# FFN activations of a decoder block turned by 16-bit transposing DMAs in place of TensorE transposes

## The chip, the cores and the metric

The kernel runs on one core of a Trainium2 chip. The metric is the time of one execution on the device, in microseconds (us), as the median of three runs. TensorE (PE) multiplies matrices, VectorE (DVE) and ScalarE (ACT) work elementwise, and the queue of SyncE (SP) and that of ScalarE issue the DMA transfers. Every engine works off its own list in the order of the program; semaphores order the engines among each other.

## The reference

One layer of a hybrid decoder for 256 positions and a model width of 2048, in float32: a mixer (dilated sliding-window attention beside a gated linear recurrence) and a SwiGLU feed-forward network (FFN), each between two RMSNorms and added to the residual stream. The part that matters here is the FFN, with D_FF = 5632:

```python
a = rmsnorm(h, norm_ffn_pre[layer])
gt, up = jnp.split(a @ w_ffn_gate_up[layer], [D_FF], axis=-1)
ff = (jax.nn.silu(gt) * up) @ w_ffn_down[layer]
h = h + rmsnorm(ff, norm_ffn_post[layer])
```

The product `silu(gt) * up` comes out with positions on the partitions. It has to be turned, so that its 5632 channels lie on the partitions, before it can be multiplied with `w_ffn_down`.

## The kernel before

**Split products.** Every float32 product is made of three in a faster format: each operand is split into a high part, rounded to that format by a ScalarE copy, and a low part, the difference, made by VectorE. Each block of weights therefore passes through raw buffers (tag `raw`, 3 buffers, loaded by SP's queue), a ScalarE copy and a VectorE subtraction before TensorE can use it. Some steps use sums of weights and of activations ("by seven", seven products where eight stand otherwise); their splitting takes more instructions: lines 434 to 449 with the sums made in place, lines 425 to 430 with sums made ahead of time and fetched from DRAM (`s<-presum`).

**Items.** The program is one list of items; an item is one step of a wide block. For item i the main loop calls `prepare(i)`, which emits the splitting of item i + 2, the fetch of sums for item i + 4 and the weight load for the raw slot five items on (its buffer comes free when the split of item i + 2 has read it), then `multiply(i)`, then pieces of the evacuations. All of it is unrolled when the program is built, so that this order is the order on each engine's list.

**Gate and up.** Block j of eleven makes 512 channels of the gate and the same 512 of up: four banks of 128 positions x 512 channels, in eight steps c = 0 to 7 (orders `GATE_UP3` and `GATE_UP4`; steps 2, 4, 5 and 6 of the latter are by seven). Each step is 21 or 24 products of 128x128 by 128x512. After the last step by seven `gather` moves the partial sums into four float32 tiles `e` (128x512 each, tag `e`, 6 buffers), `b.rest`. When the block is done, `evac_ffn` (lines 1402 to 1412) adds the banks to them, applies Silu to the gate's two and multiplies up's two by them (line 1411). The two products, one for each half of the positions, are appended to the deque `turns`. For block 0 `evac_first` does the same with tiles `g` and `u`.

**The turn.** After step c = 1 of the following gate/up block (`turn=1`; for the last product after step 3 of the first down block) the main loop calls `turn_act` (lines 1365 to 1379, from line 1653). It turns the product by eight TensorE transposes of 128x128 in float32 against an identity matrix, into two PSUM banks; ScalarE copies each bank into `act`, a slot of the pool `r` (16 slots); ScalarE's queue stores it to DRAM (`acts`). There are eleven turns. The down blocks fetch the tiles back (line 1386, 22 times 512 KB) and split them.

**Other queues.** `turns` also holds the generators that turn the mixer's output earlier in the program; the main loop tells these from the FFN's products by their type (line 1655). SP's queue carries all weight loads, the fetches of sums and the fetches of `act`, in program order; a DMA that waits for its buffer or its data holds back those behind it.

Of the kernel before, what the change touches and what calls it, by code (L numbers as in the profile page):

```python
# [14 lines left out]
F32 = mybir.dt.float32  # L15
F32R = mybir.dt.float32r
I32 = mybir.dt.int32
AF = mybir.ActivationFunctionType
OP = mybir.AluOpType

P = 128
S = 256
# [78 lines left out]
def tile_hybrid_block(ctx: ExitStack, tc: tile.TileContext, t, out):  # L101
    nc = tc.nc
# [12 lines left out]
    def nm(s):  # L115
        serial[0] += 1
        return f"{s}_{serial[0]}"

    def rslot(s):
        return rpool.tile([P, 1024], F32R, tag="r", bufs=16, name=nm(s))  # L120
# [4 lines left out]
    def aux():  # L125
        return auxp.tile([P, 512], F32, tag="aux", name=nm("aux"))

    def acc_bank():
        return accp.tile([P, 512], F32, tag="acc", name=nm("acc"))

    def p3(s, dtype, n, bufs, tag=None):
        return wide_pool[-1].tile([P, n], dtype, tag=tag or s, bufs=bufs, name=nm(s))
# [7 lines left out]
    def rsqrt_mean(dst, ss, n, bias=None):  # L140
# [6 lines left out]
        bias = bias or (eps[:, 0:1], eps[:, 1:2])  # L147
        nc.scalar.activation(y, ss, AF.Ln, scale=1.0 / n, bias=bias[0])
        nc.scalar.activation(y, y, AF.Exp, scale=-0.5)
        nc.vector.tensor_scalar(v, ss, -0.5 / n, bias[1], op0=OP.mult, op1=OP.add)  # L150
# [15 lines left out]
    ident = cpool.tile([P, P], F32, name="ident")  # L166
# [68 lines left out]
    def both_halves(ev, i):  # L235
        def go(banks):
            s = ptile("sum").rearrange("p (h t) -> p h t", h=2)
            for n, ps in enumerate(banks):
                nc.scalar.activation(s[:, n, :], ps[:, S:], AF.Copy)
            for n, ps in enumerate(banks):  # L240
# [86 lines left out]
    def ahead_of_time():  # L327

        if fp and back and not hold[0]:
            advance(back)  # L330
# [6 lines left out]
    def prepare(i):  # L337
        split(i + AHEAD)
        fetch_sums(i + AHEAD + 2)
        if i + AHEAD < len(items):  # L340
            load_upto(items[i + AHEAD][2] + N_RAW)

    def multiply(i):
        kind, n = items[i][:2]
        if kind is chunks:
            multiply_chunk(n)
            return
        b, c = steps[n][:2]

        def between():  # L350
            if b.mid:
                b.mid(c)
                prepare(i)
            advance_lanes()

        multiply_wide(n, between=between)
# [4 lines left out]
    def split_chunk(j):  # L361
        raw, w = chunks[j][2], wslot()
        chunks[j][3:] = wh, wl = w[:, :1024], w[:, 1024:]
        nc.scalar.activation(wh, raw, AF.Copy)  # L364
        nc.vector.tensor_sub(wl, raw, wh.bitcast(F32))  # L365

    def split_first(n, at):
# [5 lines left out]
        c = slice(at * 512, (at + 1) * 512)  # L373
        nc.scalar.activation(hi[:, c], raw[:, c], AF.Copy)
        nc.vector.tensor_sub(lo[:, c], raw[:, c], hi[:, c].bitcast(F32))
# [25 lines left out]
    def split_wide(n):  # L401
# [5 lines left out]
        if (b, i) == spare:  # L407
            hi = p3("spare", F32R, 2048, 1, "sum")
            lo = Joined(p3("spare", F32R, 1536, 4, "d"), p3("spare", F32R, 512, 4, "d"))
            nc.scalar.activation(hi, raw, AF.Copy)  # L410
            for c in (slice(0, 1536), slice(1536, 2048)):
# [94 lines left out]
    def gather(b):  # L506

        e = {k: p3("e", F32, 512, 6) for k in ((0, 1), (1, 1), (0, 0), (1, 0))}
        x = b.bank
        nc.scalar.activation(e[0, 1], x["p1"], AF.Copy)  # L510
        nc.vector.tensor_add(e[1, 1], x["p6"], e[0, 1])
        nc.vector.tensor_add(e[0, 0], x["p5"], e[1, 1])
        nc.vector.tensor_add(e[1, 0], x["p7"], e[0, 0])
        nc.vector.tensor_add(e[1, 1], x["p7"], e[1, 1])
        b.rest = e
# [129 lines left out]
        return row[:, None, :].to_broadcast([P, n, S])  # L645

    evacs, turns, lanes, queue = deque(), deque(), [deque(), deque()], deque()
    back, hold = deque(), [False]
    ready = set()

    def advance(q):
        if q:
            try:
                next(q[0])
            except StopIteration:
                q.popleft()
                return

    def flush(q):
        while q:  # L660
            advance(q)
# [3 lines left out]
    def advance_lanes():  # L665
        tick[0] += 1
        for lane in lanes:
            if not lane and queue:
                lane.append(attention())
            advance(lane)  # L670
# [305 lines left out]
    def recurrence(half):  # L976
# [31 lines left out]
        def on_diagonal(c, ps):  # L1008
            nc.vector.copy_predicated(
                at[:, c * 512 : (c + 1) * 512].rearrange("p (e t) -> p e t", e=4),  # L1010
                ident[:, None, :].to_broadcast([P, 4, P]).bitcast(I32),
                ps.rearrange("p (e t) -> p e t", e=4),
# [25 lines left out]
        for lev, w in enumerate(LEVELS):  # L1038
# [10 lines left out]
            if w < 32:  # L1049
                nc.vector.copy_predicated(  # L1050
                    at[:rows].rearrange("p (e n w) -> p e n w", e=8, w=2 * w)[:, :, :, w:],
                    lmask[:rows, lev, :].rearrange("p (n w) -> p n w", w=w)[:, None, :, :]
                    .to_broadcast([rows, 8, 64 // w, w]).bitcast(I32),
                    ps[:rows].rearrange("p (e n w) -> p e n w", e=8, w=w),
# [305 lines left out]
    def eslot(s="e"):  # L1360
        return p3(s, F32, 512, 6, "e")
# [2 lines left out]

    def turn_act(u):

        x = rslot("act").bitcast(F32)
        dst = x.rearrange("p (k t) -> p k t", k=4)
        for i in range(2):
            ps = aux() if now[0].flip else acc_bank()  # L1370
            for kk in range(2):
                for s in range(2):
                    at, c = kk * S + s * P, (2 * i + kk) * P
                    nc.tensor.transpose(ps[:, at : at + P], u[s][:, c : c + P], ident)  # L1374
            nc.scalar.activation(
                dst[:, 2 * i : 2 * i + 2, :], ps.rearrange("p (k t) -> p k t", k=2), AF.Copy
            )
        act_t.append(dram.tile([P, 1024], F32, name=nm("acts")))
        nc.scalar.dma_start(act_t[-1], x)

# [8 lines left out]
    now = [None]  # L1389

    def evac_first(b):
        while "r2" not in ready:
            yield
        g, u = ([eslot(n) for _ in range(2)] for n in ("g", "u"))
        for s in range(2):
            nc.scalar.activation(g[s], b.bank[s, 0], AF.Silu, scale=r2c[:, s : s + 1])
        yield
        for s in range(2):
            nc.vector.tensor_mul(u[s], b.bank[s, 1], g[s])
        turns.append(u)  # L1400

    def evac_ffn(b):
        e, x = b.rest, b.bank
        for key in ((0, 0), (0, 1), (1, 0), (1, 1)):
            nc.vector.tensor_add(e[key], x[key], e[key])
            s, g = key
            if g == 0:
                nc.scalar.activation(e[key], e[key], AF.Silu, scale=r2c[:, s : s + 1])
        yield
        for s in range(2):  # L1410
            nc.vector.tensor_mul(e[s, 1], e[s, 1], e[s, 0])
        turns.append([e[0, 1], e[1, 1]])


    fss, fz, fpost, parts_of, a7 = [], {}, [], {}, {}
# [153 lines left out]
    for half in range(2):  # L1569
        for g in range(3):  # L1570
            c = 1024 * g + 512 * half
# [24 lines left out]
    w = t["w_ffn_gate_up"][0]  # L1596
    spare = None
    add_wide_block(w, (0, FF), PLAIN, lambda k: hT[0](k), None, evac_first, True, mid=more_h)
    spare = wides[-1], 0
    for j in range(1, 11):  # L1600
        add_wide_block(w, (512 * j, FF + 512 * j), GATE_UP4 if j > 1 else GATE_UP3, lambda k: hT[0](k),
                       lambda m: h7[m], evac_ffn, j % 2 == 0,
                       pre=begin_wides if j == 1 else None, turn=1)
# [22 lines left out]
    for i in range(len(items)):  # L1626
        kind, n, _ = items[i]
        b, c = kind[n][:2]
        wide = kind is steps
        if wide:  # L1630
            now[0] = b
        if c == 0 and b.pre:
            b.pre()
        if not wide and n in items_pre:
            items_pre[n]()
        if together <= i < together + 5:
            if i == together:
                flush(evacs)
                mix_to_ffn(i)
            continue  # L1640
        if not (wide and b.mid):
            prepare(i)
        if i >= len(items) - 3:
            continue
        multiply(i)
        if b.post:
            b.post(c)
        if wide and c == b.last7:
            gather(b)
        advance(evacs)  # L1650
        if wide and c == b.turn:
            flush(evacs)
            turn_act(turns.popleft())
        for _ in range(2):
            if turns and type(turns[0]) is not list:
                advance(turns)
        advance_lanes()
        if not wide:
            ahead_of_time()
        if c == (len(b.order) if wide else b.steps) - 1:  # L1660
            evacs.append(b.evac(b if wide else b.banks))
            if wide:
                advance(evacs)
# [63 lines left out]
```

## Time and profile before

| what | value |
|---|---|
| median of three runs | 1697.17 us (1697.14 to 1698.39) |
| profiled execution, from the first to the last instruction (its span; its own time beyond that isn't given) | 1695.7 us |
| granted TensorE clock, mean | 0.998 |
| DMA, mean over the span | 244 GB/s, 413.49 MB |
| line 1374, TensorE transposes | 88 of 270 to 273 ns |
| line 1375, ScalarE copies of the turned banks | 22, median 594 to 596 ns |
| line 1379, stores of the turned tiles | 11 of 512 KB |
| line 1411, the products of gate and up, on VectorE | 20 (blocks 1 to 10), 684 ns |
| line 287, loads of gate/up weights | 156 of 512 KB and 20 of 256 KB |

The profile gives, for each engine, the instructions by source line with their shapes, and for each group the idle time of the engine just before it and what ended that idle time ("<-PE aux L138": an instruction of TensorE, line 138, that wrote a tile called `aux`). PEld is TensorE's loading of the stationary operand, which runs beside the products. "SPq" and "ACTq" are the DMA issues of these engines' queues; the time to landing of a DMA runs from its issue to its last byte. The chain that ended last is followed backwards from the end: at each step to what released an instruction, or to the one before it on the same engine. Matmuls overlap, so that one which takes 390 ns in its row may start 227 ns after the one before.

### The profile page before, as it was taken

The numbers are of one execution on the slowest core, as the hardware profiler recorded it, in microseconds if no ns is written. First come the engines' busy times: TensorE is split into PE (matmuls) and PEld (weight loads), VectorE is DVE, ScalarE is ACT, GpSimd is POOL, SyncE is SP. The second block draws the span as 40 slices with busy tenths as digits, with TensorE's granted clock in tenths as the row PEclk, the third lists the DMA queues.
The fourth block names the chain that finished last, engine by engine and source line by source line (L and its number), as shares of the span: only waits on it lengthen the run. The fifth ranks groups of instructions, "written<-read, shape, count | busy, mean of one in ns | idle before, by whom it ended". The sixth has DMA issues, their size and how long they took to land.

```text
span 1695.7 us, 21719 instructions
## 1 busy us (share of the span) xinstructions
PE 1684.4 (99%) x8257; PEld 1415.9 (83%) x8257; DVE 1416.2 (84%) x1623; ACT 945.6 (56%) x1080; POOL 3.8 (0%) x13
## 2 busy tenths in 40 slices
PE   9999999999999999999999999999999999999997
PEld 7888888888888888888888888888888888888886
DVE  6999888867978987776668888888888888898987
ACT  6655555544455555555545547555555555665653
POOL 0000000000000000000000000000000000000000
PEclk9999999999999999999999999999999999999999
DMA  8567666669677766788857646777777777777673
GB/s 286 204 224 243 231 232 229 234 216 316 228 250 256 261 239 215 259 310 279 291 171 276 208 165 226 270 249 251 255 254 255 250 248 272 252 269 259 238 255 130
DMA packets 228905, 413.49 MB, mean 244 GB/s; under 512 B 12816, under 2 KB 79552, under 8 KB 226240
## 3 DMA queue, kind: packets, MB, share of 16 engines
q1 hardware_dynamic: 218544, 373.93, 65.6%
q10 hardware_dynamic: 10192, 38.15, 5.9%
q8 instruction: 64, 1.05, 0.3%
q14 instruction: 41, 0.34, 0.1%
q0 software_dynamic: 64, 0.02, 0.0%
HBM read 376.92 MB, written 35.13 MB: 243 GB/s over the span
## 4 chain that ended last, share of the span: by engine, by line
PE 98%; DVE 1%; ACT 0%; issue 0%; DVEq 0%; ACTq 0%
PE acc L138 62%; PE aux L138 34%; PE aux L943 0%; PE aux L610 0%; PE aux L1374 0%; DVE fz L1501 0%; PE acc L1374 0%; DVE wl L420 0%; ACT junk L1455 0%; PE aux L597 0%; DVE e L1451 0%; ACT w L418 0%; PE aux L1136 0%; PE aux L1246 0%; DVE yT L578 0%
## 5 line engine op out<-in xcount | busy, mean ns | idle before, releaser
L138 PE MATMUL acc<-xT,w 128*128 128x256 f32 (+1 forms) x2048 | 365.1, 338 | 0.0
L420 DVE TENSOR_TENSOR wl<-raw,w 128x2048 fp32r<-128x2048 f32 (+1 forms) x140 | 304.6, 2183 | 70.5 <-ACT w L418 68.7
L138 PEld LDWEIGHTS acc<-xT,w 128*128 128x128 f32 x2048 | 311.9, 188 | 44.7
L365 DVE TENSOR_TENSOR w<-raw,w 128x1024 fp32r<-128x1024 f32 x176 | 215.1, 1223 | 118.1 <-ACT w L364 117.5
L418 ACT ACTIVATE w<-raw 128x2048 fp32r<-128x2048 f32 (+1 forms) x140 | 254.6, 1827 | 104.4 <-PE aux L138 33.6
L364 ACT ACTIVATE w<-raw 128x1024 fp32r<-128x1024 f32 x176 | 185.8, 1058 | 191.9 <-PE acc L138 135.8
L138 PE MATMUL acc<-w,xT 128*128 128x512 f32 x578 | 168.8, 391 | 0.0
L439 ACT ACTIVATE w<-sum 128x1024 fp32r<-128x1024 f32 x57 | 60.6, 1062 | 184.8 <-DVE sum L434 177.6
L138 PE MATMUL acc<-w,hT 128*128 128x512 f32 x472 | 152.7, 391 | 0.4 <-DVE hT L1258 0.4
L447 DVE TENSOR_TENSOR wl<-sum,w 128x1024 fp32r<-128x1024 f32 x114 | 137.2, 1221 | 12.8 <-ACT w L439 12.8
L138 PEld LDWEIGHTS acc<-w,xT 128*128 128x128 f32 x578 | 108.2, 188 | 22.2
L138 PE MATMUL aux<-w,hT 128*128 128x512 f32 x374 | 120.0, 389 | 0.0
L449 DVE TENSOR_TENSOR dl<-raw,dh 128x1536 fp32r<-128x1536 f32 x57 | 100.1, 1757 | 14.3 <-ACT dh L445 13.0
L138 PE MATMUL aux<-w,xT 128*128 128x512 f32 x344 | 109.8, 389 | 0.0
L138 PEld LDWEIGHTS acc<-w,hT 128*128 128x128 f32 x472 | 88.5, 188 | 19.0 <-DVE hT L1258 0.9
L138 PE MATMUL acc<-wl,hT 128*128 128x512 f32 x236 | 91.9, 389 | 0.0
L445 ACT ACTIVATE dh<-raw 128x1536 fp32r<-128x1536 f32 x57 | 84.1, 1476 | 8.0 <-PE aux L138 4.4
L138 PE MATMUL acc<-w,a 128*128 128x512 f32 x268 | 83.6, 389 | 0.0
L138 PEld LDWEIGHTS aux<-w,hT 128*128 128x128 f32 x374 | 70.2, 188 | 14.5
L138 PE MATMUL acc<-w,so 128*128 128x512 f32 x240 | 80.8, 391 | 0.0
L138 PE MATMUL aux<-w,a 128*128 128x512 f32 x254 | 79.4, 389 | 0.0
L138 PEld LDWEIGHTS aux<-w,xT 128*128 128x128 f32 x344 | 64.6, 188 | 13.4
(299 smaller groups left out, 2976.2 us busy)
## 6 DMA issues: line engine op xcount, KB each, us to landing
raw<-in_w_in SPq DMA_DIRECT2D x270, 512.0 KB, 4.8
raw<-in_w_ffn_gate_up SPq DMA_DIRECT2D x156, 512.0 KB, 4.9
raw<-in_w_ffn_down SPq DMA_DIRECT2D x88, 512.0 KB, 5.5
pre<-in_w_ffn_gate_up SPq DMA_DIRECT2D x40, 512.0 KB, 6.5
presum<-pre ACTq DMA_DIRECT2D x20, 1024.0 KB, 4.7
s<-presum SPq DMA_DIRECT2D x40, 512.0 KB, 6.9
raw<-in_w_mix_out SPq DMA_DIRECT2D x32, 512.0 KB, 4.8
act<-acts SPq DMA_DIRECT2D x22, 512.0 KB, 6.6
```

The source lines that it names most:

```text
L138: nc.tensor.matmul(ps, lhsT, rhs, start=start, stop=stop, skip_group_check=True)
L364: nc.scalar.activation(wh, raw, AF.Copy)
L365: nc.vector.tensor_sub(wl, raw, wh.bitcast(F32))
L418: nc.scalar.activation(hi[:, c], raw[:, c], AF.Copy)
L420: nc.vector.tensor_sub(lo[:, c], raw[:, c], hi[:, c].bitcast(F32))
L439: nc.scalar.activation(hi[:, :1024], s[:, :1024], AF.Copy)
L445: nc.scalar.activation(dhi, d, AF.Copy)
L447: nc.vector.tensor_sub(lo[:, c], s[:, c], hi[:, c].bitcast(F32))
L449: nc.vector.tensor_sub(dlo, d, dhi.bitcast(F32))
```

## The change

`turn_act` uses TensorE and PSUM no longer. A float32 word is taken as two 16-bit halves. ScalarE copies the halves of each product, viewed as unsigned 16-bit numbers, apart: into the gate's two tiles, which have been read by then, so that the first 512 columns hold one half of every word and the next 512 the other. Four transposing DMAs on SP's queue, 128 partitions x 512 halves (128 KB) each, write them turned into the product's own two tiles, one tile for each half of the words. Two steps later ScalarE joins the halves in `act`, and the store follows as before. For this `turn_act` becomes a generator with two bare yields, which a new deque `turned` advances once per step; the evacuations append a pair of lists (the tiles to be reused and the product), and the test in the main loop asks for a tuple.

```diff
+U16 = mybir.dt.uint16
...
-    back, hold = deque(), [False]
+    back, turned, hold = deque(), deque(), [False]
...
     def turn_act(u):

+        flat, turned = u
+        for s in range(2):
+            nc.scalar.activation(
+                flat[s].bitcast(U16).rearrange("p (z c) -> p z c", z=2),
+                turned[s].bitcast(U16).rearrange("p (c z) -> p z c", z=2), AF.Copy,
+            )
+        for s in range(2):
+            for z in range(2):
+                nc.sync.dma_start_transpose(
+                    turned[z].bitcast(U16).rearrange("p (k t) -> p k t", k=4)[:, :, s * P : (s + 1) * P],
+                    flat[s].bitcast(U16)[:, z * 512 : (z + 1) * 512],
+                )
+        yield
+        yield
         x = rslot("act").bitcast(F32)
-        dst = x.rearrange("p (k t) -> p k t", k=4)
-        for i in range(2):
-            ps = aux() if now[0].flip else acc_bank()
-            for kk in range(2):
-                for s in range(2):
-                    at, c = kk * S + s * P, (2 * i + kk) * P
-                    nc.tensor.transpose(ps[:, at : at + P], u[s][:, c : c + P], ident)
-            nc.scalar.activation(
-                dst[:, 2 * i : 2 * i + 2, :], ps.rearrange("p (k t) -> p k t", k=2), AF.Copy
-            )
+        words = x.bitcast(U16).rearrange("p (n z) -> p z n", z=2)
+        for z in range(2):
+            nc.scalar.activation(words[:, z, :], turned[z].bitcast(U16), AF.Copy)
         act_t.append(dram.tile([P, 1024], F32, name=nm("acts")))
         nc.scalar.dma_start(act_t[-1], x)
...
-        turns.append(u)
+        turns.append((g, u))
...
-        turns.append([e[0, 1], e[1, 1]])
+        turns.append(([e[0, 0], e[1, 0]], [e[0, 1], e[1, 1]]))
...
         if wide and c == b.turn:
             flush(evacs)
-            turn_act(turns.popleft())
+            turned.append(turn_act(turns.popleft()))
+        advance(turned)
         for _ in range(2):
-            if turns and type(turns[0]) is not list:
+            if turns and type(turns[0]) is not tuple:
                 advance(turns)
```

## The prediction

> **What bounds the kernel now.** I read the page first (busy shares, then the chain that ended last), then one window over the stage of the change, then that stage's lines.
>
> ```profile
> span 1695.7 us, 21719 instructions
> PE 1684.4 (99%) x8257; PEld 1415.9 (83%) x8257; DVE 1416.2 (84%) x1623; ACT 945.6 (56%) x1080; POOL 3.8 (0%) x13
> PE 98%; DVE 1%; ACT 0%; issue 0%; DVEq 0%; ACTq 0%
> 1087.00:1478.00 391.00, 391.00 (x1768) 324.63 (x1767) 343.32 (x307) 227.20 (x201) 0.00 (x0) 1.00 0.75 255
> ```
>
> The first three lines are the page's: TensorE is busy for 99% of the span and holds 98% of the chain. The fourth is the gate/up stage by windows (busy time of PE, PEld, DVE, ACT, POOL; granted clock; DMA share; GB/s). TensorE never pauses there, at full clock; VectorE works 343 of 391 us (88%), ScalarE 227 (58%), the DMA engines 75%. A microsecond taken off TensorE's list is therefore a microsecond off the time, as long as the split weights are still ready when TensorE asks for them.
>
> **What is removed.** The rows of line 1374, then four pieces of the chain in order of time around one turn (start, length, what):
>
> ```profile
> L1374 PE MATMUL aux<-ident,e x48: 270/272/273, 1090.3 to 1477.1; 128*128 128x128 f32 x48
> L1374 PE MATMUL acc<-ident,e x32: 270/272/273, 1132.0 to 1382.9; 128*128 128x128 f32 x32
> L1374 PE MATMUL acc<-ident,u x8: 270/272/273, 1047.9 to 1048.6; 128*128 128x128 f32 x8
> 1162.92 10.88 PE acc L138 x48
> 1173.81 0.87 PE aux L1374 x8
> 1174.68 2.06 PE aux L138 x9
> 1176.74 2.04 PE acc L138 x9
> ```
>
> There are 48 + 32 + 8 = 88 transposes, eight in each of 11 turns. One lasts 272 ns, but they overlap: eight hold the chain for 0.87 us, and the nine products behind them take 2.06 us where nine others take 2.04. So a turn costs 0.87 + 0.02 = 0.89 us, and eleven cost **9.8 us**. That is all that TensorE can give back: the 48 products ahead of them run at 10.88 / 48 = 0.227 us each, without a gap.
>
> **What is added on ScalarE.** First its rows around this turn, then VectorE's, then the DMA issues on SP's queue, and last TensorE's first use of the weights made by VectorE's 1190.99 row:
>
> ```profile
> 1168.45 1.92 ACT L418 ACTIVATE w<-raw 128x2048 fp32r<-128x2048 f32 x1 [0.86 <-ACT dh L429]
> 1174.28 1.09 ACT L1375 ACTIVATE act<-aux 128x512 f32<-128x512 f32 x2 [3.91 <-PE aux L1374]
> 1175.77 1.06 ACT L439 ACTIVATE w<-sum 128x1024 fp32r<-128x1024 f32 x1 [0.40 <-DVE sum L441]
> 1179.07 1.99 ACT L426 ACTIVATE w<-s 128x1024 fp32r<-128x1024 f32 x2
> 1180.97 1.47 ACT L429 ACTIVATE dh<-raw 128x1536 fp32r<-128x1536 f32 x1
> 1186.12 1.06 ACT L439 ACTIVATE w<-sum 128x1024 fp32r<-128x1024 f32 x1 [3.69 <-DVE sum L434]
> 1189.47 1.49 ACT L445 ACTIVATE dh<-raw 128x1536 fp32r<-128x1536 f32 x1 [0.88 <-PE aux L138]
> 1190.86 3.70 ACT L418 ACTIVATE w<-raw 128x2048 fp32r<-128x2048 f32 x2
> ...
> 1169.30 1.28 DVE L1411 TENSOR_TENSOR e<-e,e 128x512 f32<-128x512 f32 x2
> 1172.71 1.22 DVE L434 TENSOR_TENSOR sum<-raw 128x1024 f32<-128x1024 f32 x1
> 1176.86 2.36 DVE L447 TENSOR_TENSOR wl<-sum,w 128x1024 fp32r<-128x1024 f32 x2 [1.48 <-ACT w L439]
> 1190.99 1.76 DVE L449 TENSOR_TENSOR dl<-raw,dh 128x1536 fp32r<-128x1536 f32 x1 [1.15 <-ACT dh L445]
> ...
> 1173.48 0.90 SPq L287 DMA_DIRECT2D raw<-in_w_ffn_gate_up  x2
> 1180.98 0.96 SPq L287 DMA_DIRECT2D raw<-in_w_ffn_gate_up  x2
> ...
> 1194.48 0.39 PE L138 MATMUL acc<-dl,hT 128*128 128x512 f32 x1
> ```
>
> Taking apart is two copies of 1024 halves per partition, joining two more. No 16-bit copy is in the trace. Nearest is the pair of 128x1024 copies at 1179.07, 1.99 us; I take 2.0 us a pair. Bounds: half that if narrow elements run faster, double if a step of two halves costs twice. ScalarE gains 4.0 - 1.1 = 2.9 us a turn, 32 us in all, on an engine that is 58% busy, so what counts is where the copies stand.
>
> Taking apart can start when the product is written (1169.30 + 1.28 = 1170.6; ScalarE is free at 1170.4) and ends at 1172.6. Before, ScalarE stood idle here for 3.91 us, waiting for TensorE's transposes. The copy is free, and the copy of the sums (line 439, 1175.77) starts when its sums are there (1172.71 + 1.22 = 1173.9), 1.8 us earlier; VectorE at 1176.86 waited 1.48 us for just that, so the chain of splits moves about 1.4 us forward. Double price: 1174.8, still no later than before.
>
> Joining is issued two steps later, behind the dh copy of 1180.97, which ends at 1182.4, or 1181.0 after the shift. ScalarE was then idle for 3.69 us: 2.0 us of joining lie in that gap, **if the transfers have landed**. The store of the result moves along; its first reader (line 1386) comes much later:
>
> ```profile
> L1386 SPq DMA_DIRECT2D act<-acts x22: 411/466/943, 1423.9 to 1651.9; - x22
> ```
>
> **The added wait.** ScalarE runs in order, so behind a late join stand the copies of lines 439, 442 and 445 and, through them, VectorE's lo parts. From the end: TensorE takes the dl of this step at 1194.48, so at 1193.6 with 0.89 us gone. Behind line 445 stand 1.48 + 1.76 us, so it must start by 1190.3. Lines 439 and 442 need 2.0 us between them and joining 2.0, so the join must start by **1186.2**. Before that nothing is lost; after it, each late microsecond stalls TensorE in that turn.
>
> **The transfers.** SP issues the four behind the weight load of 1173.48, so from 1173.48 + 0.90 = 1174.4, by when their data is ready. That leaves 1186.2 - 1174.4 = 11.8 us. Behind them on SP's queue stands the load of 1180.98, which waited for a raw buffer: 6.6 us of the queue are empty. That load is split at 1190.86, some 5 us after it lands. The trace shows no transposing transfer. Nearest rows (KB each, us to landing), and SP's queue of the page:
>
> ```profile
> acts<-act ACTq DMA_DIRECT2D x11, 512.0 KB, 6.5
> raw<-in_w_ffn_gate_up SPq DMA_DIRECT2D x156, 512.0 KB, 4.9
> raw<-in_w_ffn_gate_up SPq DMA_DIRECT2D x20, 256.0 KB, 3.1
> out_dram<-fz SPq DMA_DIRECT2D x2, 64.0 KB, 1.7
> q1 hardware_dynamic: 218544, 373.93, 65.6%
> ```
>
> Let t be what one of the four adds to the row of four, by issue or by movement, whichever is slower. From below: 373.93 MB in 65.6% of 16 engines' 1695.7 us is 21 GB/s per engine, so 128 KB is 0.39 us; an issue on SP takes 0.45 (0.90 / 2). From above, as 512 rows of 256 bytes, each at the queue's mean price of a packet (65.6% x 16 x 1695.7 / 218544 = 81 ns): 2.6 us, and 5.2 if reading and writing are paid one after the other. To 4t comes a tail of 1.7 to 3.1 us, say 2.2, so the limit is t = (11.8 - 2.2) / 4 = **2.4 us**, and each turn is late by 4 x (t - 2.4) beyond it. I take the row closest in bytes and nature, the 512 KB store from SBUF: four issues, 1.8 us, and 6.5 to landing give 1182.7, 3.5 us before the limit (t near 1). The cost is then nothing; the cover is ScalarE's gap and the loads' 5 us.
>
> The Trainium skill speaks on both sides. VectorE: DVE Perf Modes (The three transpose paths) gives 1309 ns for a 128x128 block of 16 bits by DMA and 390 ns by TensorE, and advises TensorE where PSUM will do as destination; four blocks one after another would be t = 5.2 us, the slow rival below. For TensorE this trace shows less than the page, 0.87 / 8 = 0.11 us in the stream. DMA: Bandwidth & Descriptors (Latency and other measured facts) gives 261 GB/s for transposing DMAs, an estimate of t = 0.5 us and of the full gain. No run so far shows which holds.
>
> **Sum.** 1695.7 - 9.8 = 1685.9 us of span. The page gives only the span of the profiled execution; the median, 1697.17, lies 1.5 us above it, and I carry that: **1687.4 us**.
>
> **Rivals.**
> - **Forecast:** t at most 2.4 us, all hidden: 1687.4 (1685.5 to 1690 with the rounding of rows). For it: a free queue for 6.6 us, a ScalarE gap that opens where copies are added. Chance 0.62.
> - **Partly late:** t from 2.4 to 3.3, for which the packet price of 2.6 speaks. Late by 4 x 0.2 = 0.8 us a turn at 2.6, which eats the gain (1697.2 - 9.8 + 8.8 = 1696.2), and by 3.6 at 3.3 (1727). Chance 0.16.
> - **Slower, the transfers become the bound of a turn:** t = 5.2. The join starts 11.2 us late and TensorE stands still for it eleven times: 1697.2 - 9.8 + 123 = 1810. It decides from t = 2.6 on. For it: the DMA engines are 75% busy in this stage, and nothing shows how fast a transposed write is. Against it: the tail of 11.8 us is long for 512 KB. Chance 0.16.
> - **No gain though TensorE's list is shorter:** VectorE at 343 of then 381 us (90%) sets the pace: 1697. Against it: splits are ready 1.7 us before use (1190.99 + 1.76 against 1194.48) and the change takes a wait out of VectorE's chain. Chance 0.04.
> - **The change doesn't do what it says:** the transfers fall into single halves of words. 65536 packets at 81 ns on 16 engines are 332 us a transfer, 44 of them over 14 ms. Chance 0.02.
>
> **How the numbers follow.** A difference under 0.2%, 3.4 us, can't be told from no change. Faster: the forecast and t up to 2.55, 0.62 + 0.03. Within: t of 2.55 to 2.7 and the VectorE case, 0.03 + 0.04. Slower: the rest of the partly late case, the slow rival and single halves, 0.10 + 0.16 + 0.02. The range takes the forecast, the partly late case and the VectorE case (0.82): 1685.5 to 1727.
>
> **What would show it.** Right: line 1374 gone, 88 fewer matmuls; the chain runs from the 48 products into the next nine without a piece between; the splits' line 439 early in a turn starts near 1174; the joins start without a long idle before them, or with one that ends by some 1186 in this turn's clock. Wrong: the join's ACT rows show idle time ended by a DMA of several us, TensorE shows idle time ended by dl or wl once a turn, or SP's queue shows transposing issues of over 2 us with the next weight load behind them. If taking apart takes much over 2 us a pair, my copy price was wrong, and the limit of 1186.2 moves forward by the excess of the join.

## The result and the profile after

The changed kernel takes 1688.77 us (median of four runs, 1687.57 to 1689.89) against 1697.16 us for the kernel before: a ratio of 0.9949, 95% interval 0.9935 to 0.9963, so 0.4 to 0.65% faster. The forecast was 1687.4, range 1685.5 to 1727. A second series of five runs gave 1689.57 against 1697.62, ratio 0.9948 (0.9935 to 0.9962).

The page of the changed kernel, its span, engines and SP's queue. Line numbers have moved by one up to the change: the products are line 139, line 440 was 439.

```profile
span 1688.1 us, 21672 instructions
PE 1674.2 (99%) x8169; PEld 1406.0 (83%) x8169; DVE 1416.6 (84%) x1623; ACT 983.1 (58%) x1102; POOL 3.9 (0%) x13
q1 hardware_dynamic: 242480, 379.70, 68.1%
```

The window of the gate/up stage (columns as before):

```profile
1087.00:1470.00 383.00, 382.81 (x1689) 316.65 (x1689) 344.85 (x309) 260.72 (x222) 0.00 (x0) 1.00 0.86 272
```

TensorE has 88 instructions fewer and 10.2 us less work, VectorE the same, ScalarE 37.5 us more. SP's queue has 242480 - 218544 = 23936 more packets, 544 for each of 44 transfers, for 5.8 MB more. TensorE still works without pause (382.8 of 383.0 us), but the DMA engines' share in the stage has risen from 0.75 to 0.86.

The chain in order of time around the fourth turn, the one shown before:

```profile
1161.79 10.88 PE acc L139 x48
1172.67 2.04 PE aux L139 x9
1174.71 2.04 PE acc L139 x9
```

1161.79 + 10.88 = 1172.67: the piece of 0.87 us is gone, and the nine products behind it take 2.04 instead of 2.06 us. The same turn in the timeline of ScalarE:

```profile
1167.31 1.92 ACT L419 ACTIVATE w<-raw 128x2048 fp32r<-128x2048 f32 x1 [0.86 <-ACT dh L430]
1169.14 1.99 ACT L1370 ACTIVATE e<-e 128x1024 uint16<-128x1024 uint16 x2
1172.88 1.06 ACT L440 ACTIVATE w<-sum 128x1024 fp32r<-128x1024 f32 x1 [1.76 <-DVE sum L435]
...
1178.52 1.48 ACT L430 ACTIVATE dh<-raw 128x1536 fp32r<-128x1536 f32 x1
1181.51 2.59 ACT L1385 ACTIVATE act<-e 128x1024 uint16<-128x1024 uint16 x2 [1.52 <-DMA e<-e]
1184.56 1.06 ACT L440 ACTIVATE w<-sum 128x1024 fp32r<-128x1024 f32 x1 [0.46 <-DVE sum L441]
1187.44 1.49 ACT L446 ACTIVATE dh<-raw 128x1536 fp32r<-128x1536 f32 x1 [0.86 <-PE aux L139]
1188.83 3.71 ACT L419 ACTIVATE w<-raw 128x2048 fp32r<-128x2048 f32 x2
```

And in that of SP's queue:

```profile
1172.95 6.92 SPq L1376 DMA_TRANSPOSE e<-e  x4
1179.97 3.39 SPq L288 DMA_DIRECT2D raw<-in_w_ffn_gate_up  x4
```

Taking apart (line 1370) fills the gap in which ScalarE waited for TensorE, and line 440 now waits for VectorE's sums alone. Joining (line 1385) waits 1.52 us for the transfers, but ends in time: line 446 behind it still waits for TensorE, as it did before. On SP's queue the four transfers take 6.9 us, and the next weight load goes out 0.1 us behind them.

**Where the time went.** I compared the start of each TensorE product, transposes left out, in the trace of before and in that of after, and noted where the difference jumps:

| place | jump, us |
|---|---|
| start of the program (TensorE waits for the first pieces of x) | +1.07 |
| each of the eleven turns, the last one behind the start of the down stage | -0.89 |
| sixth and seventh step of the first block with a turn | +0.47 |
| first products of the down stage | +0.47 |
| smaller ones behind | -0.04 |
| sum | -7.85 |

The first row lies in the opening, where the kernels have the same code. Against before, the traces of the ten other kernels below lie there between 0.75 us earlier and 0.6 us later, and that of the changed kernel's second series 1.8 us later. I take it for chance, which is not shown; both profiled executions of the changed kernel were the slowest of their series. From the first turn on the gain is 8.9 us of the 9.8 forecast. The 0.47 us in the first block with a turn are a wait: there the fetch of sums stands behind the transfers on SP's queue, goes out at 1057.60 (1051.56 before) and holds up ScalarE, VectorE and TensorE in turn (timeline of the changed kernel, all engines):

```profile
1057.60 2.09 SPq L326 DMA_DIRECT2D s<-presum  x2
...
1065.60 1.06 ACT L427 ACTIVATE w<-s 128x1024 fp32r<-128x1024 f32 x1 [0.35 <-DMA s<-presum]
...
1068.06 1.76 DVE L431 TENSOR_TENSOR dl<-raw,dh 128x1536 fp32r<-128x1536 f32 x1
...
1069.88 0.50 PE L139 MATMUL aux<-dl,hT 128*128 128x512 f32 x1
```

At the down stage TensorE waits for VectorE to clear its banks. VectorE has worked without a pause there since a wait for the copy of line 440, which stands behind the last join of the gate/up stage:

```profile
1432.03 2.36 DVE L448 TENSOR_TENSOR wl<-sum,w 128x1024 fp32r<-128x1024 f32 x2 [2.20 <-ACT w L440]
...
1447.57 0.47 PE L139 MATMUL acc<-w,a 128*128 128x512 f32 x1 [0.19 <-DVE e L1413]
```

### The profile page after: what moved, and what is told of

It is laid out like the page before. It is cut to its first block, busy times and chain, and to the rows that moved or that the text cites. A ratio compares the mean times of both kernels' runs of the same rounds, so it can differ in the third digit from the quotient of the medians.

```text
span 1688.1 us, 21672 instructions
## 1 busy us (share of the span) xinstructions
PE 1674.2 (99%) x8169; PEld 1406.0 (83%) x8169; DVE 1416.6 (84%) x1623; ACT 983.1 (58%) x1102; POOL 3.9 (0%) x13
## 3 DMA queue, kind: packets, MB, share of 16 engines
q1 hardware_dynamic: 242480, 379.70, 68.1%
## 4 chain that ended last, share of the span: by engine, by line
PE 95%; DVE 2%; ACT 1%; DMA 1%; issue 1%; SPq 0%; DVEq 0%; ACTq 0%
PE acc L139 62%; PE aux L139 32%; DVE wl L421 1%; PE aux L944 0%; DMA raw<-in_w_ffn_gate_up 0%; ACT w L419 0%; DMA x<-in_x 0%; PE aux L611 0%; DVE fz L1509 0%; DVE dl L431 0%; ACT junk L1463 0%; PE aux L598 0%; DVE e L1459 0%; DVE wl L428 0%; DVE f L543 0%
```

## The experiments

Every kernel is the changed one with one edit.

**The transposes put back.**

```diff
+        for i in range(2):
+            ps = aux() if now[0].flip else acc_bank()
+            for kk in range(2):
+                for s in range(2):
+                    at, c = kk * S + s * P, (2 * i + kk) * P
+                    nc.tensor.transpose(ps[:, at : at + P], turned[s][:, c : c + P], ident)
         for s in range(2):
             for z in range(2):
                 nc.sync.dma_start_transpose(
```

> The changed kernel (1688.8 us) with the eight TensorE transposes of each turn put back beside the transfers; their results are read by nobody. Theory (the gain is only the 0.89 us that a turn's transposes hold TensorE): 11 x 0.89 = 9.8 us come back, 1698.6. Rival (part of the gain comes from ScalarE and VectorE no longer waiting for TensorE's transposes at the start of a block): less than that comes back, 1692 to 1696, because ScalarE's copy of the sums still starts early.

Measured: 1698.02 us, ratio to before 1.0005 (0.9996 to 1.0015). The chain of this kernel around the fourth turn:

```profile
1162.55 10.88 PE acc L139 x48
1173.43 0.87 PE aux L1379 x8
1174.31 2.06 PE aux L139 x9
```

The piece of 0.87 us is back, and product by product this kernel falls behind the changed one by 0.89 us in each of the eleven turns; the two losses of 0.47 us are not there, though the transfers are. So the whole gain is TensorE's time; ScalarE's earlier start is worth nothing by itself.

**No transfers.** The 44 transfers are left out, and the join reads what was taken apart:

```diff
-        for s in range(2):
-            for z in range(2):
-                nc.sync.dma_start_transpose(
...
-        words = x.bitcast(U16).rearrange("p (n z) -> p z n", z=2)
-        for z in range(2):
-            nc.scalar.activation(words[:, z, :], turned[z].bitcast(U16), AF.Copy)
+        words = x.bitcast(U16).rearrange("p (s n z) -> p s z n", s=2, z=2)
+        for s in range(2):
+            nc.scalar.activation(
+                words[:, s], flat[s].bitcast(U16).rearrange("p (z n) -> p z n", z=2), AF.Copy
+            )
```

> The changed kernel without the 44 transposing transfers: halves are taken apart and joined again at the same places by the same four ScalarE copies, and nothing is turned, so that part of the computation is left out. Theory (the transfers are hidden from the second turn on, and cost TensorE under 1 us in all, most of it in the first gate/up block with a turn, where a fetch of sums stands behind them on SP's queue): 1687.9, no idle time of TensorE between the first turn and the end of the gate/up stage. Rival (they cost something in each turn by holding up weight loads or crowding the DMA engines): 1680 to 1685.

Measured: 1687.69 us, ratio to before 0.9941 (0.9924 to 0.9958). Against the changed kernel the products gain 0.45 us at the sixth and seventh step of the first block with a turn and 0.47 where the down stage begins; in the turns between there is no jump of 0.15 us or more. The transfers cost about 0.9 us in all, and nothing in turns three to ten.

**The join one step earlier, and one step later.**

```diff
 early:
-        yield
 late:
+        yield
         x = rslot("act").bitcast(F32)
```

> The changed kernel with joining one step after taking apart instead of two, so that ScalarE comes to the join some 5 us before the transfers land and all splitting behind it waits. Theory (a late join is paid by TensorE beyond some 3 us): the low part of the next step by seven is ready 4.2 us late by the rows, ten turns, 1688.8 + 42 = 1731. Rival (VectorE and ScalarE catch up, as buffers hold three steps): under 1695.

> The changed kernel with joining three steps after taking apart instead of two. Theory (ScalarE's wait at the join, 15.7 us in nine turns, lies in its idle time and costs nothing, and the copies behind the later place have over 1 us to spare): the wait for the transfers goes to 0, the time stays at 1688.8 within 1 us. Rival (that wait is what is missing between the 9.8 us forecast and the 8.4 measured): 1687.4.

Early: 1762.62 us, ratio 1.0381 (1.0360 to 1.0402); the theory's direction, but not its size (1731). TensorE's idle time is what the theory said: 44.9 us between 1000 and 1735 us of its trace, 0.8 in the same part of the changed kernel, where 42 were expected. The rest is a slower clock behind these stalls, which the last section shows. Late: 1698.47 us, ratio 1.0004 (0.9994 to 1.0013): the theory failed. The wait for the transfers is gone, yet all of the gain is lost. ScalarE in the late kernel, one turn and the start of the down stage:

```profile
1190.52 2.56 ACT L1386 ACTIVATE act<-e 128x1024 uint16<-128x1024 uint16 x2
1193.53 3.72 ACT L419 ACTIVATE w<-raw 128x2048 fp32r<-128x2048 f32 x2 [0.46 <-ACT act L1386]
1199.63 1.93 ACT L419 ACTIVATE w<-raw 128x2048 fp32r<-128x2048 f32 x1 [1.89 <-DMA raw<-in_w_ffn_gate_up]
...
1450.03 1.91 ACT L419 ACTIVATE w<-raw 128x2048 fp32r<-128x2048 f32 x1 [3.95 <-DMA raw<-in_w_ffn_down]
```

VectorE's low part behind the first of these splits, and TensorE's first product of the down stage:

```profile
1195.48 4.49 DVE L421 TENSOR_TENSOR wl<-raw,w 128x2048 fp32r<-128x2048 f32 x2 [3.08 <-ACT w L419]
...
1455.01 0.77 PE L139 MATMUL acc<-w,a 128*128 128x512 f32 x1 [4.35 <-DVE e L1414]
```

The 2.6 us of the join now stand ahead of a split (line 419). VectorE waits 3.08 us for that split, its low part comes late, and TensorE's product that takes it starts late (1197.83): TensorE loses about 0.4 us in most turns and 0.8 in each of the first two. At the start of the down stage it loses 6.3 us more than the changed kernel: a DMA wait of 3.95 us delays what VectorE does before it clears TensorE's banks, TensorE stands still for 4.35 us, and the clock is slower behind that. The load that ScalarE waits for went out at 1439.73 and 1440.14 and took 8.8 and 9.7 us to land; the same load of the changed kernel took 4.8 and 5.7. The store of the joined tile goes out just behind it here (1440.41), well ahead of it there; whether that is what held it was not tried.

**Three unread transfers more, ahead of the four or behind them.** They go into buffers that are dead by then; those behind are issued after the four.

```diff
+        for q, d in ((0, lambda: p3("spare16", U16, 512, 1)), (1, lambda: warm.bitcast(U16)), (2, lambda: rowb.bitcast(U16))):
+            nc.sync.dma_start_transpose(
+                d().rearrange("p (k t) -> p k t", k=4),
+                flat[q % 2].bitcast(U16)[:, q // 2 * 512 : (q // 2 + 1) * 512],
+            )
```

> The changed kernel with three more transposing transfers per turn of the same 128 KB, into buffers that nobody reads, issued ahead of the four. At 1.7 us each on SP's queue the four land 5 us later. Theory (a join may end some 3.1 us later than it does now before TensorE waits): 1.9 us late in each of ten turns and some 5 us in the first block with a turn, where a fetch of sums stands behind: 1688.8 + 24 = 1713, with ScalarE idle before the join for 6 us. Rival (movement, not issue, sets the landing; landings now lie 0.5 us apart): the four land 1.5 us later, about 1690 beside the first block.

> The changed kernel with the same three extra transfers per turn issued behind the four, so that the join is not late but the next weight load on SP's queue goes out 5 us later. Theory (the load has some 5 us between landing and use, TensorE another 2): nothing lost in the ten later turns, some 5 us in the first block with a turn: 1694. Rival (SP's queue is the tight place, not the join): as slow as with the three ahead, 1710 or more.

Ahead: 1720.98 us, ratio 1.0137 (1.0106 to 1.0167). Behind: 1718.10 us, ratio 1.0120 (1.0090 to 1.0149). The theory's 1713 for the first was near, its 1694 for the second wrong: by the time the rival held, and it hardly matters whether the three stand ahead or behind. With the three behind, the timeline of SP's queue in the fourth turn:

```profile
1181.21 7.13 SPq L1376 DMA_TRANSPOSE e<-e  x4
1188.38 1.27 SPq L1381 DMA_TRANSPOSE spare<-e  x1
...
1192.37 2.77 SPq L288 DMA_DIRECT2D raw<-in_w_ffn_gate_up  x4
```

And those of ScalarE and TensorE:

```profile
1190.18 2.60 ACT L1390 ACTIVATE act<-e 128x1024 uint16<-128x1024 uint16 x2 [1.92 <-DMA e<-e]
1199.25 1.92 ACT L419 ACTIVATE w<-raw 128x2048 fp32r<-128x2048 f32 x1 [2.63 <-DMA raw<-in_w_ffn_gate_up]
...
1198.47 0.50 PE L139 MATMUL acc<-dl,hT 128*128 128x512 f32 x1 [0.99 <-DVE dl L450]
```

Two weight loads go out together behind the transfers, and the split of the first then waits 2.63 us for its DMA. That is not where TensorE loses in this turn: it waits 0.99 us for the `dl` behind the join, and in the other turns too mostly for `dh` or `dl`. For the join is late here as well. TensorE's products run 4.9 us later at this point than in the changed kernel; beyond these 4.9 us the product of the turn is written 3.2 us late, the transfers begin 3.4 us late and the join 3.8 us late. The split ahead of the product on VectorE is late by the same 3.2 us (line 421, at 1166.43 against 1158.33), so the lateness comes from the turn before; the product is late by 2.3 to 3.4 us in each of the turns three to ten.

**Eight transfers of half the size.**

```diff
+                for h in range(2):
                     nc.sync.dma_start_transpose(
-                    turned[z].bitcast(U16).rearrange("p (k t) -> p k t", k=4)[:, :, s * P : (s + 1) * P],
-                    flat[s].bitcast(U16)[:, z * 512 : (z + 1) * 512],
+                        turned[z].bitcast(U16).rearrange("p (k t) -> p k t", k=4)[
+                            :, 2 * h : 2 * h + 2, s * P : (s + 1) * P
+                        ],
+                        flat[s].bitcast(U16)[:, z * 512 + h * 256 : z * 512 + (h + 1) * 256],
```

> The changed kernel with each transfer cut into two of 128x256 halves of words, eight per turn of 64 KB, the same bytes and the same rows of 256 bytes. An issue now takes SP's queue 1.22 to 2.40 us, median 1.6. Theory 1 (the issue's time goes with the rows): 0.6 to 0.8 us each, the time stays at 1688.8 within 1 us. Theory 2 (the issue's time is fixed per transfer): eight of over 1.2 us, the last lands some 4 us later, 1688.8 + 10 to 24 = 1699 to 1713.

Measured: 1715.46 us, ratio 1.0104 (1.0075 to 1.0133): theory 2. The issues of the changed kernel, then those of this one (count: minimum, median and maximum in ns):

```profile
L1376 SPq DMA_TRANSPOSE e<-e x40: 1217/1610/2399, 1093.5 to 1476.8; - x40
```

```profile
L1377 SPq DMA_TRANSPOSE e<-e x80: 1182/1244/2297, 1097.2 to 1504.7; - x80
```

SP's timeline in the fourth turn of the latter:

```profile
1182.63 11.23 SPq L1377 DMA_TRANSPOSE e<-e  x8
```

Half the size takes a floor of 1.18 us where the full size takes 1.22. The bytes are those of the changed kernel and the time is 27 us more.

**Two transfers of double size, alone and with the three unread ones behind them.**

```diff
+        both = rslot("turn").bitcast(F32)
         for s in range(2):
-            for z in range(2):
-                nc.sync.dma_start_transpose(
-                    turned[z].bitcast(U16).rearrange("p (k t) -> p k t", k=4)[:, :, s * P : (s + 1) * P],
-                    flat[s].bitcast(U16)[:, z * 512 : (z + 1) * 512],
-                )
+            nc.sync.dma_start_transpose(
+                both.bitcast(U16).rearrange("p (k t) -> p k t", k=8)[:, :, s * P : (s + 1) * P],
+                flat[s].bitcast(U16),
+            )
...
-            nc.scalar.activation(words[:, z, :], turned[z].bitcast(U16), AF.Copy)
+            nc.scalar.activation(words[:, z, :], both.bitcast(U16)[:, z * 1024 : (z + 1) * 1024], AF.Copy)
```

> The changed kernel with two transfers of 128x1024 halves of words (256 KB) per turn in place of four of 128x512, into one slot of the pool r. Theory (an issue takes SP's queue 1.2 us or more whatever its size; moving takes 0.5 us per 128 KB): SP is held some 3 us a turn instead of 7, the last still lands near 8 us after the first issue, because weight loads stand ahead in the queue; the 0.9 us lost at the first turn and at the end of the stage shrink to 0.3 or less: 1688.0, 0.5 us below the changed kernel. Rival (the issue's time goes with the bytes above some size): issues of 2.5 us or more, time as the changed kernel's.

> The two large transfers per turn, with the three unread transfers of 128 KB behind them: five issues and 896 KB, where the changed kernel has four and 512 KB and the kernel with three behind has seven and 896 KB (1718). Theory (SP's queue time decides, five issues of 1.3 to 1.7 us): as the changed kernel plus a little, 1688 to 1692. Rival (the bytes on the DMA engines decide): as the kernel with three behind, over 1712.

> The changed kernel once more, for a closer time. By its trace eleven turns give back 0.89 us each and about 0.9 us is lost again at three places (the first turn, the second and the end of the gate/up stage): 8.9 us less than before, some 1688.5. Rival (something outside the turns costs too): 8 us less or under.

Alone: 1688.80 us, ratio to before 0.9949 (0.9937 to 0.9961), beside 1689.57 for the changed kernel in the same series: no difference that can be told. SP is held as long as with four, so the theory's 3 us did not come; the rival's signs did. The loss in the first block with a turn is gone, and the one at the start of the down stage is 1.2 us. With three more: 1711.98 us, ratio 1.0084 (1.0065 to 1.0102); near the rival's figure, and again not issues of 1.3 to 1.7 us. The changed kernel once more came out 8.05 us below before, with an interval from 6.5 to 11.0, which settles neither 8.9 nor the rival's 8; by its trace the gain from the first turn on is 8.8 us. The issues of the two large ones, in the later turns and in the first:

```profile
L1376 SPq DMA_TRANSPOSE turn<-e x20: 2037/3466/4308, 1089.5 to 1472.9; - x20
L1376 SPq DMA_TRANSPOSE turn<-g x2: 1346/1532/1717, 1050.8 to 1052.2; - x2
```

SP's timeline in the fourth turn:

```profile
1170.95 7.20 SPq L1376 DMA_TRANSPOSE turn<-e  x2
```

In the first turn 256 KB are issued in 1.35 to 1.72 us; in later turns an issue takes 3.5 us, and two hold SP as long as four of half the size do. There the issue is not held by its own work. The likeliest reason is that the queue has room only as the 2 MB of loads issued just ahead are moved, but no run took those loads away.

**What these times go with** is how long SP's queue is held by a turn's transfers, here in the fourth turn, from the start of the first issue to the end of the last:

| kernel | transfers, KB in a turn | SP held, us | time, us |
|---|---|---|---|
| changed | 4, 512 | 6.9 | 1688.8, 1689.6 |
| two of double size | 2, 512 | 7.2 | 1688.8 |
| two of double size, three behind | 5, 896 | 11.1 | 1712.0 |
| eight of half size | 8, 512 | 11.2 | 1715.5 |
| four, three behind | 7, 896 | 11.1 | 1718.1 |
| four, three ahead | 7, 896 | 11.7 | 1721.0 |

Some 7 us cost about 1 us, 11 to 12 us cost 22 to 32. The bytes do not order the times, the third and fourth rows above all, and neither does the number of transfers. Within the last four rows the time held does not order them either. There TensorE's idle time from 1000 us on and half of its time at half clock (last section) make 21, 26, 25 and 29 us, row by row.

**The transfers on ScalarE's queue.**

```diff
-                nc.sync.dma_start_transpose(
+                nc.scalar.dma_start_transpose(
```

> The changed kernel with its transfers issued by ScalarE's queue instead of SP's. Theory (an issue holds its engine as long as it held SP, 1.6 us): ScalarE stands still for some 6.5 us right before the copy of the sums, the low part of the last step by seven comes about 2.6 us late in ten turns, 1688.8 + 26 = 1715. Rival (the issue runs beside ScalarE's copies, and SP's queue is free): 1688 to 1689, and the first block with a turn loses nothing.

Measured: 1734.97 us, ratio 1.0219 (1.0189 to 1.0249). ScalarE in a turn:

```profile
1177.39 10.24 ACTq L1376 DMA_TRANSPOSE e<-e  x4
1187.73 1.06 ACT L440 ACTIVATE w<-sum 128x1024 fp32r<-128x1024 f32 x1 [9.42 <-issue]
```

The issues hold ScalarE as they held SP, and longer, 10.2 us for four; its next copy waits 9.4 us behind them. The theory's direction, at 46 us instead of 26. TensorE's idle time, 27.0 us between 1000 and 1708 us of the trace, is what the theory said; a slower clock behind the stalls comes on top here too.

## Why the prediction was right, and where its steps were off

**The gain.** 0.89 us a turn was right: all eleven turns show it to 0.01 us, and putting the transposes back takes it away again.

**The copies.** Taking apart was forecast at 2.0 us a pair in ScalarE's gap and took 1.99 there. Joining took 2.59 instead of 2.0; the gap held that as well. ScalarE's work grew by 37.5 us where 32 were forecast.

**The price of a transfer.** I took t near 1 us. It came out as two prices. By movement, the four of the fourth turn land between 1172.95 + 7.54 = 1180.49 and 1178.29 + 3.78 = 1182.07 (times to landing of the first and the last in the trace), so 0.53 us apart, near the bound from bytes (0.39). By issue, they hold the queue for 6.92 / 4 = 1.73 us each, where I had set the 0.45 us of a plain issue as the measure. The larger price was that of SP's queue, and it was under the limit of 2.4. The forecast of the landing, 8.3 us after the first issue begins, was near the 9.1 measured, but by luck: 1.8 us of issues and 6.5 to landing were put in where 5.3 and 3.8 came out. One sign that was named for a failure did show: an issue of over 2 us (the third, 2.22) with the next weight load right behind the four. The load had room, and nothing was lost.

On the two figures of the Trainium skill: 0.53 us for 128 KB is 247 GB/s, which is near the 261 GB/s of DMA: Bandwidth & Descriptors (Latency and other measured facts). The Trainium skill's 1309 ns for a block, in VectorE: DVE Perf Modes (The three transpose paths), does not add up block by block: a transfer holds four such blocks and lands 0.53 us behind the one before. It is close to what one issue takes here in the first turn, 1.25 to 1.30 us, with 0.75 MB of loads on their way ahead of it; in the fourth turn 2 MB were.

**The limit and its cover.** The join's limit was placed at 1186.2 by the clock of before, which is 1184 to 1185 here; the join starts at 1181.51, so the room was there. And the path behind the join was right. The changed kernel's `dl` of this turn is written at 1188.96 + 1.76 = 1190.72 and used at 1192.45, so 1.7 us are left; where the join starts 3.8 us later, with three transfers behind, TensorE waits 0.99 us for that `dl`.

The step that failed is the other half of the cover, "the loads' 5 us". That was read from one load. The next one has less: in the changed kernel its second half is issued at 1182.89, takes 6.2 us to land, at 1189.1, and is split as the second of the two copies that start at 1188.83, at about 1190.6. That leaves 1.5 us, and the load just behind the transfers now goes out the moment the queue is free. The three transfers behind the four and the eight halves used up this room by SP's queue; the join one step later put a split late on ScalarE. They lost 9 to 29 us. With this the prediction also failed to see that lateness is carried on: it takes each turn by itself, with transfers that start at a fixed time, while a late load makes the next turn's product, its transfers and its join late. For the three transfers behind the four its formula, with t unchanged, gives no loss, and 29 us were measured; for an average of 11.1 / 4 = 2.8 us it gives 4 x 0.4 x 11 = 18 us, where 22 to 32 were measured. No run holds SP's queue for between 7.2 and 11 us in this turn, so where the limit lies is open. No run gave the loads more room either, by a fourth raw buffer for instance, so the loop of raw buffer, split and next load is read from the traces and not shown by an experiment.

**The slow rival** named the right mechanism, transfers that become the bound of a turn, and placed its price at t = 5.2; at 1.73 it did not come about. That VectorE would set the pace did not either: TensorE is busy for all but 0.2 us of the stage.

**What is missing** to the 9.8 us is 0.9 us, half in the first block with a turn and half at the start of the down stage, which goes when the transfers are left out; the rest of the 1.4 us between forecast and median lies within what single executions differ by. The order on SP's queue in the first block with a turn was not looked at in the prediction: I read one turn in the middle and took it for all eleven.

## What to carry to other kernels

Moving work from the engine that bounds a kernel to a DMA queue pays if the queue's own list has a hole as long as the issues take, not as long as the bytes take; count each transfer's issue by its measured time, and look at the load that stands behind the load behind it. A wait on an in-order engine is harmless only up to the next thing it feeds, so follow the buffers around their whole loop, into the next turn, before calling a gap free. Read the first and the last turn as well as one in the middle: what is lost was lost there.

## What the runs showed of the hardware

An issue of a transposing DMA holds the engine that issues it for at least 1.2 us whether it moves 64 KB (1182 ns at least) or 128 KB (1217 ns), and 1.35 us for 256 KB, where a plain weight load's issue of 512 KB took 0.45 us; in a later turn, behind loads on their way, one of 256 KB took up to 4.3 us.

A stall of TensorE can cost more than its length. The kernel with the late join by windows around its stall of 4.35 us (the column after POOL's is the granted clock):

```profile
1448.00:1451.00 3.00, 2.66 (x12) 1.88 (x10) 2.82 (x5) 0.97 (x1) 0.00 (x0) 1.00 0.90 295
1451.00:1455.00 4.00, 0.00 (x0) 0.02 (x1) 3.27 (x4) 1.04 (x2) 0.00 (x0) 0.73 0.98 327
1455.00:1457.00 2.00, 1.99 (x5) 1.63 (x6) 1.65 (x3) 1.51 (x3) 0.00 (x0) 0.50 0.85 288
1457.00:1459.00 2.00, 2.00 (x7) 1.54 (x6) 0.22 (x1) 1.99 (x3) 0.00 (x0) 0.50 0.95 325
```

For 4.7 us behind the stall, up to 1459.7, the clock is granted at half, and the products start 0.43 us apart instead of 0.23, which adds about 2.3 us. The kernel with the early join pays this over and over. One window from before its first turn to behind its last, and three around one of its stalls:

```profile
1000.00:1735.00 735.00, 690.07 (x2922) 558.34 (x2921) 593.35 (x583) 438.32 (x408) 0.00 (x0) 0.97 0.73 235
1208.00:1211.00 3.00, 0.35 (x3) 0.01 (x1) 2.85 (x4) 2.67 (x4) 0.00 (x0) 1.00 0.73 281
1211.00:1217.00 6.00, 4.98 (x11) 3.64 (x12) 5.96 (x3) 3.94 (x3) 0.00 (x0) 0.50 0.53 180
1217.00:1220.00 3.00, 3.00 (x12) 2.43 (x12) 2.13 (x4) 0.20 (x1) 0.00 (x0) 0.85 1.02 348
```

In the long window the clock is granted at half for 51.2 us in all, in ten stretches; in the same part of the changed kernel it never is. An estimate from this, as if TensorE had worked through all of it: half of 51.2 us, 25.6, and the 44.2 us more of idle time make 70 of the 74 us by which it is slower than the changed kernel. The same sum gives 38 of 46 us for the transfers on ScalarE's queue (23.9 us at half clock) and 28 of 32 us for the three transfers ahead (20.5 us).
